# Four weight loads on ScalarE's queue and an input norm on VectorE alone, in the first stage of a two-layer hybrid attention trunk

## The chip, the cores and the metric

The kernel runs on one core of a Trainium2 chip. The metric is the device time of one execution in microseconds, and the median of several executions stands for a kernel. One execution was also taken by the hardware profiler; it has a time of its own beside its span (from the first to the last instruction on the core).

## The reference

The reference computes a two-layer trunk over 512 latent tokens and 256 context tokens of width 2048. What matters here is the head of layer 0:

```python
mod = silu_c @ w_mod[l] + b_mod[l]                     # c -> shift, scale, gate
shift, scale, gate = jnp.split(mod[:, None, :], 3, axis=-1)
h = rmsnorm(x, norm_g[l]) * (1.0 + scale) + shift       # the same for the context tokens, with c_ctx
u = h @ e_w_in[i]                                       # input projection, then the mixers
...
x = x + gate * (y @ w_o[l])
```

So no column of `h` can be made before the piece of `mod` that shifts and scales it, and `w_mod` is large: the shift and scale parts of layer 0 alone are 2048 x 4096 floats (33.6 MB).

## The kernel before, in words

Activations lie transposed: 16 chunks `k` of 128 features, each a tile of 128 partitions by 768 tokens (512 latent, 256 context). Every fp32 product is made of three matmuls on split operands: `wsplit` casts a piece of weights to a high part `wh` on ScalarE (L265), and VectorE makes the rest, `wl` (L224, the function `sub`); `make_h` does the same with an activation, giving `h` and `l`.

The first stage, which the change touches, works through eight groups `g` of 256 modulation columns:

- `mod_first(g)` loads the weights of group `g` in 11 pieces (`mraw`, L147; ten of 384 KB and one of 256 KB), multiplies each on TensorE into a bank (L151), copies the bank (L157, ScalarE), adds the four row strips on TensorE (L160), and `mod_finish` writes the columns `modc` on VectorE (L125, L129).
- `make_h(0, k, ...)` for the two chunks `k = 2g, 2g+1`: `xn = xT[k] * rs0` (L353), then the shift and scale on ScalarE (L358, makes `h`) and on VectorE (L361, in place in `xn`), then `l` (L224). In L353 GpSimd (POOL) does the ten chunks with `k % 3` not zero, VectorE (DVE) the six others. There are three buffers for `xn`, so `xn` of chunk `k` needs the `l` of chunk `k-3` to be done.
- The projection of four blocks of 128 output columns (`start_cols`) runs along with it, chunk by chunk: `mm_step` (L284, L285, L287). TensorE's order is written out by hand: in each pass `g` of the loop stand eight `mm_step`s; behind the first one group `g+1` is finished and its two `h` are begun, and behind each of the last four stand the matmuls of 3, 3, 3 and 2 pieces of group `g+2`. I call these four places the slots of a group.

Every load is issued by SP, the common queue (`nc.sync`), and SP issues in order: an issue that waits for a buffer holds all behind it. A scheduler orders the instructions of the engines other than TensorE. The `mraw` pieces lie in two kinds of buffers. Groups 0 to 4 use a pool of 32 tiles (`hslot`) that are free at the start. The later pieces of groups 5 and 6 use the tiles of the pool `s3` in which the inputs `xT[2]` to `xT[11]` lie at the start (`slot`); such a piece can be loaded only when L353 has read its `xT[k]`. The scheduler set these pieces early among the loads of groups 1 to 5.

The four weight blocks are loaded by `start_loads(k)` in two halves, `k = 0` and `k = 8`, four loads of 512 KB each (three `wraw`, and one into the buffer `macc`), L274:

```python
            if g == 2:
                with tc.issue_after(last_raw[0].ins):
                    start_loads(8)
```

Behind the stage come the heads of layer 0. There VectorE also sums further modulation columns (L179, `mod_later`), whose loads (L172) are on SP too.

Of the kernel before, what the change touches and what calls it, by code (L numbers as in the profile page):

```python
# [12 lines left out]
ALU = mybir.AluOpType  # L13
# [4 lines left out]
P = 128  # L18
# [23 lines left out]
def trunk_kernel(ctx: ExitStack, tc: tile.TileContext, T):  # L42
    nc = tc.nc
# [21 lines left out]
    def slot(name):  # L65
        return sp["s3"].tile([P, TOK], F32, tag="s3", name=name)
# [10 lines left out]
    def tmp(name):  # L77
        return sp["tm"].tile([P, TOK], F32, tag="tmp", name=name)

    def hslot(name, dt=F32R):  # L80
        return hp.tile([P, TOK], dt, tag="hT", name=name)
# [50 lines left out]
    last_raw = [None]  # L132

    def mod_first(g):

        acc = pst.tile([P, 512], F32, name="T")
        for r0 in range(0, 32, 3):
            n = min(3, 32 - r0)

            i = r0 // 3  # L140
            if i < (11, 11, 11, 11, 11, 6, 4, 3)[g]:
                raw = hslot("mraw0", F32)
            elif g == 7 and i > 8:
                raw = wp.tile([P, 1024], F32, name="mraw", bufs=2)
            else:
                raw = slot("mraw0")
            last_raw[0] = nc.sync.dma_start(raw[:, :n * 256], T["wm0"][g][:, r0 * 256:(r0 + n) * 256])  # L147
            for i in range(n):
                sec, at = divmod(r0 + i, NCH)
                j = at % 4  # L150
                nc.tensor.matmul(acc[32 * j:32 * j + 32, 256 * sec:256 * sec + 256], lhsT=sil[:, at, :],  # L151
                                 rhs=raw[:, 256 * i:256 * i + 256], start=(at < 4), stop=(at >= NCH - 4),
                                 tile_position=(0, 32 * j))
            if r0 + n < 32:
                yield
        asb = sp["ep"].tile([P, TOK], F32, name="e")[:, 0:512]
        nc.scalar.copy(asb, acc)  # L157
        yield
        for i in range(4):
            nc.tensor.matmul(acc[:, 2 * i:2 * i + 2], lhsT=asb[:, P * i:P * i + P], rhs=sel, start=True, stop=True)  # L160
        for sec in range(2):
            mod_finish(0, 2 * g + NCH * (1 - sec), 2, acc[:, 4 * sec:4 * sec + 4].rearrange("p (c v) -> p c v", c=2))
        yield
# [28 lines left out]
    def shift(l, k, v):  # L192
        return modc[l][:, k, v:v + 1]

    def ascale(l, k, v):
        return modc[l][:, NCH + k, v:v + 1]
# [26 lines left out]
    def sub(o, a, h):  # L223
        nc.vector.tensor_tensor(o, a, h.bitcast(F32), op=ALU.subtract)  # L224
# [19 lines left out]
    def rstd_cols(accs, ts, dim, name, bank=jbank):  # L244

        mp = bank()
        steps = [(a, t) for a in accs for t in ts]
        for i, (a, t) in enumerate(steps):
            nc.tensor.matmul(mp[:, 2 * t:2 * t + 2], lhsT=a[:, P * t:P * t + P], rhs=ones[:, 0:2],  # L249
                             start=(i == 0), stop=(i == len(steps) - 1))  # L250
        rs = sm.tile([P, 12], F32, name=name, bufs=2)
        n = 2 * len(ts)
        nc.scalar.activation(rs[:, :n], mp[:, :n], AF.Sqrt, bias=epsc, scale=1.0 / dim)
        nc.vector.reciprocal(rs[:, :n], rs[:, :n])
        return rs


    def wsplit(rv, nk):

        res = []  # L260
        for k0 in range(0, nk, 4):
            n = min(4, nk - k0)
            wh = wp.tile([P, 4, P], F32R, name="wh", bufs=4)
            wl = wp.tile([P, 4, P], F32R, name="wl", bufs=4)
            nc.scalar.copy(wh[:, :n, :], rv[:, k0:k0 + n, :])  # L265
            sub(wl[:, :n, :], rv[:, k0:k0 + n, :], wh[:, :n, :])
            res += [(wh[:, i, :], wl[:, i, :]) for i in range(n)]
        return res

    def wraw(w, col, k0, nk, raw=None):  # L270

        if raw is None:
            raw = wp.tile([P, 1024], F32, name="wraw", bufs=3)
        nc.sync.dma_start(raw[:, :nk * P], w[col // P][:, k0 * P:(k0 + nk) * P])  # L274
        return raw[:, :nk * P].rearrange("p (k c) -> p k c", k=nk)

    def mm_step(lat, cx, wk, xk, first, last, opens=True, closes=True, at=(0, 512)):


        wh, wl = wk  # L280
        xh, xl = xk
        regs = [(lat, *at)] + ([(cx, 512, 768)] if cx is not None else [])
        for o, c0, c1 in regs:
            nc.tensor.matmul(o, lhsT=wh, rhs=xh[:, c0:c1], start=first and (opens or o is lat), stop=False)  # L284
            nc.tensor.matmul(o, lhsT=wh, rhs=xl[:, c0:c1], start=False, stop=False)  # L285
        for o, c0, c1 in regs:
            nc.tensor.matmul(o, lhsT=wl, rhs=xh[:, c0:c1], start=False, stop=last and (closes or o is lat))  # L287

    def proj(w, col, xs=None, lat_only=False, at=(0, 512)):
        xs = hT if xs is None else xs  # L290
        n = len(xs)
        lat = psj.tile([P, 512], F32, name="J")[:, :at[1] - at[0]]
        cx = None if lat_only else psj.tile([P, 512], F32, name="J")[:, :256]
        for k0 in range(0, n, 8):
            nk = min(8, n - k0)
            ws = wsplit(wraw(w, col, k0, nk), nk)
            for i in range(nk):
                mm_step(lat, cx, ws[i], xs[k0 + i], k0 + i == 0, k0 + i == n - 1, at=at)
        return lat, cx
# [7 lines left out]
    for k in range(NCH):  # L307
        xk = hslot("xT", F32) if k == 0 else tmp("xT") if k == 1 else slot("xT") if k < 12 else (oslot if k < 14 else sgslot)("xT")
# [41 lines left out]

    def make_h(l, k, xk, rs, xn, first):

        (nc.gpsimd if k % 3 else nc.vector).tensor_tensor(xn, xk, rs, op=ALU.mult)  # L353
        h = hslot(f"h{l}_{k}")
        lo = hslot(f"l{l}_{k}")
        for v, c0, c1 in halves:
            a = ascale(l, k, v) if first == "norm" else 1.0
            nc.scalar.activation(h[:, c0:c1], xn[:, c0:c1], AF.Identity, bias=shift(l, k, v), scale=a)  # L358
        for v, c0, c1 in halves:
            if first == "norm":  # L360
                nc.vector.tensor_scalar(xn[:, c0:c1], xn[:, c0:c1], ascale(l, k, v), shift(l, k, v),  # L361
                                        op0=ALU.mult, op1=ALU.add)
            else:
                nc.vector.scalar_tensor_tensor(lo[:, c0:c1], xn[:, c0:c1], shift(l, k, v), h.bitcast(F32)[:, c0:c1],  # L364
                                               op0=ALU.add, op1=ALU.subtract)
        if first == "norm":
            sub(lo, xn, h)
        return h, lo


    w = T["ew"]
    s_start = sbanks()
    o_start = pso.tile([P, 512], F32, name="O")
    start_cols = (A_K0, A_Q0, A_V0, E_G0)
# [5 lines left out]
    raws = [None] * 4  # L380

    def start_loads(k):

        for i in range(4):
            raw = sm.tile([P, 2, 512], F32, name="macc", bufs=1).rearrange("p a b -> p (a b)") if i == 3 else None
            raws[i] = wraw(w, start_cols[i], k, 8, raw)

    def two_h(g):
        for k in (2 * g, 2 * g + 1):
            hs[k] = make_h(0, k, xT[k], rs0, tmp("xn"), "norm")  # L390
# [3 lines left out]
    with tc.manual_schedule(engines={mybir.EngineType.PE}):  # L394
        start_loads(0)
        for _ in mod_first(0):
            pass
        two_h(0)
        nxt = mod_first(1)
        for _ in range(11):  # L400
            next(nxt)
        for g in range(NCH // 2):
            for n in range(8):
                k, i = 2 * g + n // 4, n % 4
                if k % 4 == 0:
                    ws4[i] = wsplit(raws[i][:, k % 8:k % 8 + 4, :], 4)
                mm_step(*start_ps[i], ws4[i][k % 4], hs[k], k == 0, k == NCH - 1, opens=(i % 2 == 0), closes=(i % 2 == 1))
                if n == 0 and nxt is not None:
                    for _ in nxt:
                        pass  # L410
                    two_h(g + 1)
                    nxt = mod_first(g + 2) if g < NCH // 2 - 2 else None
                if n >= 4 and nxt is not None:
                    for _ in range((3, 3, 3, 2)[n - 4]):
                        next(nxt)
            if g == 2:
                with tc.issue_after(last_raw[0].ins):
                    start_loads(8)
    with tc.issue_after(last_raw[0].ins):
        load_cs(64)  # L420
    xT = None
# [302 lines left out]
    w = T["ow"]  # L724
# [6 lines left out]
    for k in range(NCH):  # L731
        xk = slot("xk")
# [65 lines left out]
    for g in range(2):  # L798
# [9 lines left out]
        rs = rstd_cols((sq,), range(6), P, "rsx", bank)  # L808
# [262 lines left out]
```

## Time and profile before

| what | us |
|---|---|
| median of 3 runs | 2517.13 |
| lowest and highest run | 2510.58, 2518.85 |
| the profiled execution, its own time | 2515.64 |
| its span | 2513.9 |
| TensorE busy | 2408.1 (96%) |
| VectorE busy | 1570.2 (62%) |
| ScalarE busy | 1011.7 (40%) |
| GpSimd busy | 247.8 (10%) |

The profiled execution's time and its span differ by 1.74 us. A row of the timeline has the start, the busy time, the engine, the line, the operation with its output and inputs, a count of merged instructions, and in brackets the engine's idle time before it and what ended it. A row of the waits has who waited for whom, the total, the number of waits and the longest. A row of a table by stretches has the stretch, its length, the busy time of TensorE, its weight loads, VectorE, ScalarE and GpSimd with counts, the granted TensorE clock, the busy share of the 16 DMA engines, and GB/s.

### The profile page before, as it was taken

To read this page: it belongs to the slowest core of one execution; us is meant where nothing else is said; L and a number is where in the kernel's file an instruction comes from. 1 tells how busy PE (TensorE), PEld (TensorE's weight loads), DVE (VectorE), ACT (ScalarE), POOL (GpSimd) and SP (SyncE) were. 2 spreads that over 40 slices of the span, in tenths; PEclk is the share of its full clock that TensorE was granted. 3 is DMA by queue.
4 is the path that set the end of the run, shared out by engine and by line. 5 is a ranking of instruction groups with operands and counts; after the bars stand their busy time and mean duration, and the time that the engine had idled before them with its cause. 6 is when DMAs were issued, how large, how long until landed. Compare 5 with 4: busy or idle time off the path is not lost.

```text
span 2513.9 us, 36308 instructions
## 1 busy us (share of the span) xinstructions
PE 2408.1 (96%) x14234; PEld 2077.1 (83%) x14234; DVE 1570.2 (62%) x2796; ACT 1011.7 (40%) x1964; POOL 247.8 (10%) x160
## 2 busy tenths in 40 slices
PE   3898999999999999999989999899999999999998
PEld 1677888888888899989878888688888888888787
DVE  4358667556965787887566664757545336776534
ACT  3234555444454334323342222444434334554434
POOL 1111001001000011010001012200001010100010
PEclk8999999999999999999999999899999999999999
DMA  8853111111312343443325545425422221222234
GB/s 305 302 179 100 43 57 56 50 57 57 109 58 72 100 144 113 142 164 111 134 96 199 188 170 184 146 92 191 150 72 84 69 95 56 64 93 68 97 118 151
DMA packets 97931, 297.48 MB, mean 118 GB/s; under 512 B 11488, under 2 KB 12512, under 8 KB 97760
## 3 DMA queue, kind: packets, MB, share of 16 engines
q1 hardware_dynamic: 97760, 295.16, 34.7%
q8 instruction: 112, 1.84, 0.3%
q14 instruction: 59, 0.48, 0.1%
HBM read 269.16 MB, written 25.95 MB: 117 GB/s over the span
## 4 chain that ended last, share of the span: by engine, by line
PE 87%; DVE 6%; DMA 3%; issue 2%; ACT 1%; SPq 0%; ACTq 0%; DVEq 0%
PE J L284 22%; PE J L287 22%; PE J L285 22%; PE O L563 6%; PE S L505 4%; PE T L548 3%; PE S L501 3%; DMA mraw<-in_wm_dram 2%; PE T L151 1%; DVE macc L179 1%; DVE l L364 1%; PE J L187 1%; DVE wl L224 1%; PE T L249 1%; PE T L229 1%
## 5 line engine op out<-in xcount | busy, mean ns | idle before, releaser
L284 PE MATMUL J<-h,wh 128*128 128x512 f32 (+1 forms) x2224 | 789.0, 356 | 9.3 <-DVE sg L493 3.2
L285 PE MATMUL J<-l,wh 128*128 128x512 f32 (+1 forms) x2224 | 762.5, 353 | 3.6 <-DVE l L364 3.6
L287 PE MATMUL J<-h,wl 128*128 128x512 f32 (+1 forms) x2224 | 704.3, 355 | 9.2 <-DVE wl L224 9.2
L265 ACT CAST wh<-wraw 128x512 fp32r<-128x512 f32 x492 | 304.1, 620 | 682.1 <-PE J L285 581.3
L224 DVE TENSOR_TENSOR wl<-wraw,wh 128x512 fp32r<-128x512 f32 x500 | 363.7, 731 | 317.7 <-ACT wh L265 307.1
L284 PEld LDWEIGHTS J<-h,wh 128*128 128x128 f32 x2224 | 421.3, 189 | 94.3 <-issue 8.2
L285 PEld LDWEIGHTS J<-l,wh 128*128 128x128 f32 x2224 | 421.9, 190 | 56.7 <-DVE l L364 4.8
L287 PEld LDWEIGHTS J<-h,wl 128*128 128x128 f32 x2224 | 386.4, 190 | 44.1 <-DVE wl L224 12.4
L179 DVE SCALAR_TENSOR_TENSOR macc<-mraw,silc,macc 128x512 f32<-128x512 f32 x420 | 317.2, 787 | 34.6 <-DMA mraw<-in_wm_dram 31.9
L284 PE MATMUL J<-yh,wh 128*128 128x512 f32 (+1 forms) x800 | 275.3, 351 | 4.7 <-ACT yh L469 4.7
L285 PE MATMUL J<-yl,wh 128*128 128x512 f32 (+1 forms) x800 | 271.7, 350 | 1.0 <-DVE yl L224 0.9
L287 PE MATMUL J<-yh,wl 128*128 128x512 f32 (+1 forms) x800 | 253.6, 349 | 0.2 <-DVE wl L224 0.2
L517 DVE TENSOR_REDUCE nb<-S 128x1 f32<-128x768 f32 (+3 forms) x208 | 166.2, 799 | 140.0 <-PE S L505 73.0
L552 ACT CAST pth<-T 128x256 fp32r<-128x256 f32 (+2 forms) x288 | 125.0, 450 | 190.4 <-PE T L548 186.6
L284 PEld LDWEIGHTS J<-yh,wh 128*128 128x128 f32 x800 | 149.9, 189 | 31.6 <-ACT yh L469 5.5
L224 DVE TENSOR_TENSOR ptl<-T,pth 128x256 fp32r<-128x256 f32 (+2 forms) x288 | 144.2, 514 | 49.1 <-ACT pth L552 47.3
L285 PEld LDWEIGHTS J<-yl,wh 128*128 128x128 f32 x800 | 150.5, 189 | 22.3 <-DVE yl L224 3.1
L524 ACT ACTIVATE e<-S,nb 128x256 f32<-128x256 f32 (+3 forms) x144 | 104.3, 724 | 156.4 <-DVE nb L517 90.5
L287 PEld LDWEIGHTS J<-yh,wl 128*128 128x128 f32 x800 | 140.4, 189 | 13.2 <-DVE wl L224 0.5
L431 POOL TENSOR_TENSOR r<-r,cos 128x512 f32<-128x512 f32 x31 | 44.3, 1428 | 792.1 <-DVE t L430 736.2
L548 PE MATMUL T<-identr,e 128*128 128x128 f32 x784 | 116.3, 275 | 2.9 <-DVE e L534 2.6
L548 PEld LDWEIGHTS T<-identr,e 128*128 128x128 f32 x784 | 95.2, 142 | 16.7 <-issue 2.8
(283 smaller groups left out, 3143.7 us busy)
## 6 DMA issues: line engine op xcount, KB each, us to landing
mraw<-in_wm_dram SPq DMA_DIRECT2D x128, 512.0 KB, 3.7
wraw<-in_ew_dram SPq DMA_DIRECT2D x102, 512.0 KB, 3.7
wraw<-in_ow_dram SPq DMA_DIRECT2D x64, 512.0 KB, 3.6
wraw<-in_wo_dram SPq DMA_DIRECT2D x62, 512.0 KB, 3.8
mraw<-in_wm_dram SPq DMA_DIRECT2D x80, 384.0 KB, 7.4
xT<-in_xT_dram SPq DMA_DIRECT2D x16, 384.0 KB, 7.6
res<-in_xT_dram SPq DMA_DIRECT2D x16, 384.0 KB, 4.3
xad<-nx SPq DMA_DIRECT2D x16, 384.0 KB, 2.7
```

Of the source, the lines that this page charges most:

```text
L179: nc.vector.scalar_tensor_tensor(macc[:, v, :], rv[:, i, :], sc, macc[:, v, :], op0=ALU.mult, op1=ALU.add)
L224: nc.vector.tensor_tensor(o, a, h.bitcast(F32), op=ALU.subtract)
L265: nc.scalar.copy(wh[:, :n, :], rv[:, k0:k0 + n, :])
L284: nc.tensor.matmul(o, lhsT=wh, rhs=xh[:, c0:c1], start=first and (opens or o is lat), stop=False)
L285: nc.tensor.matmul(o, lhsT=wh, rhs=xl[:, c0:c1], start=False, stop=False)
L287: nc.tensor.matmul(o, lhsT=wl, rhs=xh[:, c0:c1], start=False, stop=last and (closes or o is lat))
L505: nc.tensor.matmul(S[:, 512:end], lhsT=q, rhs=k[:, 128 * lo:128 * hi], start=(i == 0), stop=(i == n - 1 and not masks))
L517: nc.vector.tensor_reduce(nb, S, axis=AX.X, op=ALU.max, negate=True)
L524: nc.scalar.activation(e, S, AF.Exp, bias=nb, scale=1.0 if scale is None else scale, accum_out=den)
L548: nc.tensor.transpose(out=tp[:, 128 * (b - b0):128 * (b - b0) + 128], in_=e[:, 128 * b:128 * b + 128], identity=ident)
L552: nc.scalar.copy(ph, tv)
L563: nc.tensor.matmul(o, lhsT=v[:, cols[i]], rhs=pt[part][:, i, :], start=(n == 0), stop=(n == len(steps) - 1))
```

## The change

It has three parts. Both calls of `start_loads` issue their four loads on ScalarE's queue. The second call no longer waits for the last piece of the modulation weights that was issued ahead of it. And L353 of the first stage (`l == 0`) is done by VectorE for all 16 chunks.

```diff
-    def wraw(w, col, k0, nk, raw=None):
+    def wraw(w, col, k0, nk, raw=None, queue=None):
...
-        nc.sync.dma_start(raw[:, :nk * P], w[col // P][:, k0 * P:(k0 + nk) * P])
+        (queue or nc.sync).dma_start(raw[:, :nk * P], w[col // P][:, k0 * P:(k0 + nk) * P])
...
-        (nc.gpsimd if k % 3 else nc.vector).tensor_tensor(xn, xk, rs, op=ALU.mult)
+        (nc.gpsimd if l and k % 3 else nc.vector).tensor_tensor(xn, xk, rs, op=ALU.mult)
...
-            raws[i] = wraw(w, start_cols[i], k, 8, raw)
+            raws[i] = wraw(w, start_cols[i], k, 8, raw, nc.scalar)
...
-                with tc.issue_after(last_raw[0].ins):
-                    start_loads(8)
+                start_loads(8)
```

The scheduler answers with another order on SP. This is SP's queue behind the loads of group 1, whose last piece is `mraw_468`; `mraw_1012` and `mraw_1023` are pieces of group 5 that go into the tiles of `xT[4]` and `xT[5]`, and `mraw_546` is the first piece of group 2:

```order
 L147 DMA mraw_468<-in_wm_dram 128x512
 L147 DMA mraw_1012<-in_wm_dram 128x768
+L147 DMA mraw_1023<-in_wm_dram 128x768
 L147 DMA mraw_546<-in_wm_dram 128x768
 L147 DMA mraw_551<-in_wm_dram 128x768
```

The piece for the tile of `xT[5]` moved ahead of the eleven loads of group 2. This is SP's queue between group 2 (last piece `mraw_614`) and group 3 (first piece `mraw_676`); `mraw_1028` goes into the tile of `xT[6]`, and `mraw_1132`, of group 6, into that of `xT[7]`:

```order
 L147 DMA mraw_609<-in_wm_dram 128x768
 L147 DMA mraw_614<-in_wm_dram 128x512
-L147 DMA mraw_1023<-in_wm_dram 128x768
 L147 DMA mraw_1028<-in_wm_dram 128x512
+L147 DMA mraw_1132<-in_wm_dram 128x768
 L147 DMA mraw_676<-in_wm_dram 128x768
 L147 DMA mraw_681<-in_wm_dram 128x768
```

The piece for `xT[7]` moved ahead of group 3, behind which it stood. And this is SP's queue between group 4 (last piece `mraw_890`) and the first pieces of group 5; `mraw_1153` and `mraw_1158` go into the tiles of `xT[10]` and `xT[11]`:

```order
 L147 DMA mraw_885<-in_wm_dram 128x768
 L147 DMA mraw_890<-in_wm_dram 128x512
-L274 DMA wraw<-in_ew_dram 128x1024 x3
-L274 DMA macc<-in_ew_dram 128x1024
 L147 DMA mraw_1153<-in_wm_dram 128x768
+L147 DMA mraw_1158<-in_wm_dram 128x768
 L147 DMA mraw_960<-in_wm_dram 128x768
 L147 DMA mraw_965<-in_wm_dram 128x768
```

The four weight loads are gone from there, and the piece for `xT[11]` moved ahead of group 5. On VectorE, this is the work around the finish of group 1 in the kernel before (`xn_491` is chunk 2, `xn_500` chunk 3):

```order
L125 TENSOR_TENSOR modc0_193<-T_417,bmod_174 128x4 x2
L129 SCALAR_TENSOR_TENSOR modc0_193<-modc0_193,vcol_173 128x4
L361 TENSOR_SCALAR xn_491<-xn_491,modc0_193 128x512
L361 TENSOR_SCALAR xn_491<-xn_491,modc0_193 128x256
L224 TENSOR_TENSOR l0_2_494<-xn_491,h0_2_493 128x768
L361 TENSOR_SCALAR xn_500<-xn_500,modc0_193 128x512
L361 TENSOR_SCALAR xn_500<-xn_500,modc0_193 128x256
L224 TENSOR_TENSOR l0_3_503<-xn_500,h0_3_502 128x768
```

And the same place now, where `xT_216` is `xT[4]` and `xT_221` is `xT[5]`:

```order
L353 TENSOR_TENSOR xn_633<-xT_216,e_276 128x768
L125 TENSOR_TENSOR modc0_193<-T_417,bmod_174 128x4 x2
L129 SCALAR_TENSOR_TENSOR modc0_193<-modc0_193,vcol_173 128x4
L361 TENSOR_SCALAR xn_491<-xn_491,modc0_193 128x512
L361 TENSOR_SCALAR xn_491<-xn_491,modc0_193 128x256
L224 TENSOR_TENSOR l0_2_494<-xn_491,h0_2_493 128x768
L361 TENSOR_SCALAR xn_500<-xn_500,modc0_193 128x512
L353 TENSOR_TENSOR xn_642<-xT_221,e_276 128x768
L361 TENSOR_SCALAR xn_500<-xn_500,modc0_193 128x256
L224 TENSOR_TENSOR l0_3_503<-xn_500,h0_3_502 128x768
```

The two L353 that GpSimd had stand among VectorE's instructions, that of chunk 5 behind the finish of group 1. Last, ScalarE's queue around the finish of group 2, where the second half of the weights is issued:

```order
L358 ACTIVATE h0_5_644<-xn_642,modc0_193 128x512
L358 ACTIVATE h0_5_644<-xn_642,modc0_193 128x256
L265 CAST wh_750<-wraw_327 128x512
L274 DMA wraw_896<-in_ew_dram 128x1024
L265 CAST wh_785<-wraw_329 128x512
L274 DMA wraw_898<-in_ew_dram 128x1024
```

Each load stands behind the cast that read its buffer last and ahead of the next cast. It waits for VectorE's `wl` of that buffer as well.

## The prediction

> **What bounds the kernel now.** I read the page's head first, then the stretches of the first stage, then SP's waits, then the timeline of TensorE and VectorE there.
>
> ```profile
> PE 2408.1 (96%) x14234; PEld 2077.1 (83%) x14234; DVE 1570.2 (62%) x2796; ACT 1011.7 (40%) x1964; POOL 247.8 (10%) x160
> 40.00:60.00 20.00, 8.60 (x60) 2.54 (x60) 4.83 (x10) 3.09 (x5) 1.80 (x1) 0.66 0.69 242
> 60.00:80.00 20.00, 18.56 (x152) 11.31 (x149) 6.43 (x10) 3.10 (x5) 2.01 (x1) 1.00 1.00 376
> 100.00:120.00 20.00, 13.99 (x94) 7.37 (x93) 3.21 (x5) 0.52 (x2) 1.80 (x1) 0.74 0.86 319
> 120.00:140.00 20.00, 20.00 (x151) 14.82 (x150) 10.79 (x20) 8.37 (x14) 2.01 (x1) 1.00 0.80 293
> ```
>
> TensorE bounds the kernel as a whole, so only time that TensorE loses or wins counts. In the stage that the change touches it loses time at two places, around 50 and around 105 us, and there its granted clock is low too (0.66 and 0.74). What ends those waits is SP's queue:
>
> ```profile
> SPq L147 <- DVE xn L353: 9.3, 1, 9.3
> SPq L147 <- DVE xn L353: 10.7, 1, 10.7
> 48.04 0.95 DVE L353 TENSOR_TENSOR xn<-xT,e 128x768 f32<-128x768 f32 x1
> 49.06 19.29 SPq L147 DMA_DIRECT2D mraw<-in_wm_dram  x24
> 100.97 0.96 DVE L353 TENSOR_TENSOR xn<-xT,e 128x768 f32<-128x768 f32 x1
> ```
>
> The first two rows are SP's waits in the stretches 39 to 50 and 90 to 104 us: SP stood 9.3 and 10.7 us at a piece of group 5 or 6 whose tile still held `xT[3]` or `xT[9]`, until VectorE's L353 of that chunk ended at 49.0 and 101.9. The loads of groups 1 and 4 stood behind. The row at 49.06 shows the opposite case: 24 issues in 19.3 us are the blocked piece, the 11 of group 1, the piece for `xT[4]`, and all 11 of group 2, so group 2 was issued by 68.35, before anything of it was needed.
>
> What a blocked group costs is read from VectorE's finish of each group and TensorE's matmuls on its pieces:
>
> ```profile
> 44.53 0.23 DVE L125 TENSOR_TENSOR modc<-T,bmod 128x4 f32<-128x4 f32 x2 [9.78 <-PE T L160]
> 66.88 0.23 DVE L125 TENSOR_TENSOR modc<-T,bmod 128x4 f32<-128x4 f32 x2 [16.57 <-PE T L160]
> 82.16 0.23 DVE L125 TENSOR_TENSOR modc<-T,bmod 128x4 f32<-128x4 f32 x2 [7.80 <-PE T L160]
> 97.45 0.23 DVE L125 TENSOR_TENSOR modc<-T,bmod 128x4 f32<-128x4 f32 x2 [2.09 <-PE T L160]
> 121.88 0.23 DVE L125 TENSOR_TENSOR modc<-T,bmod 128x4 f32<-128x4 f32 x2 [18.64 <-PE T L160]
> 137.17 0.23 DVE L125 TENSOR_TENSOR modc<-T,bmod 128x4 f32<-128x4 f32 x2 [2.04 <-PE T L160]
> 168.57 0.23 DVE L125 TENSOR_TENSOR modc<-T,bmod 128x4 f32<-128x4 f32 x2 [2.04 <-PE T L160]
> 71.00 1.48 PE L151 MATMUL T<-mraw,sil 128*32 128x256 f32 x18
> 88.95 1.48 PE L151 MATMUL T<-mraw,sil 128*32 128x256 f32 x18
> 106.36 1.95 PE L151 MATMUL T<-mraw,sil 128*32 128x256 f32 x12 [4.71 <-DMA mraw<-in_wm_dram]
> 112.84 2.00 PE L151 MATMUL T<-mraw,sil 128*32 128x256 f32 x18
> ```
>
> These are the finishes of groups 0, 1, 2, 3, 4, 5 and 7. A group whose loads came ahead takes 15.28 us (66.88 to 82.16), 15.29 (82.16 to 97.45) or 15.29 (121.88 to 137.17). The one that was blocked, group 4, takes 24.43 (97.45 to 121.88): 9.15 more. The loss is complete by the second slot: 112.84 + 2.00 is 17.39 after the finish ahead of it, where 88.95 + 1.48 is 8.27, so 9.12.
>
> **The change part by part.** First, which pieces block after the change. A load into the tile of `xT[k]` can go when L353 of chunk `k` is done. In the new order the pieces for `xT[5]`, `xT[7]` and `xT[11]` stand ahead of groups 2, 3 and 5, and those L353 stand on VectorE behind the finishes of groups 1, 2 and 4. Their place is that of chunks 3 and 9 above, between the two L361 of the chunk before. The end of L353 there is 101.93 - 97.45 = 4.48 us after the finish. Nothing can make it earlier: it needs that finish's L361 and `l` to free an `xn` buffer. In the kernel before GpSimd did these three, later still, but SP had the groups' loads out by then:
>
> ```profile
> 70.21 2.01 POOL L353 TENSOR_TENSOR xn<-xT,e 128x768 f32<-128x768 f32 x1 [18.03 <-DVE l L224]
> 125.22 2.01 POOL L353 TENSOR_TENSOR xn<-xT,e 128x768 f32<-128x768 f32 x1 [20.04 <-DVE l L224]
> ```
>
> Group 2: SP reaches its new blocker around 60 (13 issues after 49.06 instead of 24, at 19.3 / 24 = 0.8 us), waits until 66.88 + 4.5 = 71.4, and only then issues the eleven loads; TensorE wants the first three at 71.00. That is group 4's situation to the row, so I take its whole loss, +9.15. From below the loss is at least the idle time ahead of the first matmul, 4.71; from above I have only the 9.15 itself and what competes for the transfer. Group 3: the same, +9.15. Group 5: only six of its pieces stand behind the blocker, the other five having been loaded into `xT` tiles; but the loss arises in the first two slots, which are those six. Seven instead of twelve transfers run together, so I take +8.0, between 4.71 and 9.15. Groups 1 and 4 are blocked at the same chunks (3 and 9) as before: 0.
>
> Second, the first four weight loads, 2.1 MB. They leave SP's queue between `tri` and group 0 and start with the kernel.
>
> ```profile
> 16.00:18.00 2.00, 0.00 (x0) 0.00 (x0) 1.79 (x3) 1.56 (x3) 0.00 (x0) 1.00 1.03 415
> 20.00:22.00 2.00, 0.00 (x0) 0.00 (x0) 1.79 (x3) 1.56 (x3) 0.00 (x0) 1.00 0.20 37
> 24.00:26.00 2.00, 0.00 (x1) 0.01 (x1) 1.10 (x4) 0.41 (x1) 0.00 (x0) 1.00 1.01 403
> 19.61 2.96 SPq L274 DMA_DIRECT2D wraw<-in_ew_dram  x3
> 22.61 0.97 SPq L274 DMA_DIRECT2D macc<-in_ew_dram  x1
> 42.73 0.58 ACT L157 COPY e<-T 128x512 f32<-128x512 f32 x1 [10.63 <-PE T L151]
> ```
>
> The transfers were full at 415 GB/s while the inputs came, so the weights push these back by what they take themselves, 2.1 MB / 403 GB/s = 5.2 us, and group 0's loads then start where the weights' issues stood. The dip at 20 us comes from the six small loads behind the inputs, which stay. Group 0's finish is the end of the same bytes: 0, with -5.2 (the weights cost nothing early) and +4.0 (SP's 2.96 + 0.97 of issuing turn out to have been hidden, and the inputs' delay is not) as ends. The Trainium skill, page "DMA: Bandwidth & Descriptors", section "Issuing engines are not separate DMA queues", states that transfers begun by different engines run on the same 16 DMA engines and interleave, and that a second issuing engine saves only the sequencer's issue time. By that rule this term is 0 too, where a reader who counts a second queue as more bandwidth would write -5.2. The norm's factors come some 5 us later, with the inputs (4 casts and 4 `wl` now stand among the squares); VectorE idled 9.78 us ahead of group 0's finish and ScalarE 10.63 ahead of its copy at 42.73, which covers it; without that slack it would be +5.2. TensorE's six L229 behind group 0's first three pieces lie in the same slack.
>
> Third, the second half of the weights. ScalarE issues it behind the casts for chunk 4, while group 3's blocked loads come:
>
> ```profile
> 86.05 0.62 ACT L265 CAST wh<-wraw 128x512 fp32r<-128x512 f32 x1 [0.94 <-PE S L285]
> 88.71 0.62 ACT L265 CAST wh<-wraw 128x512 fp32r<-128x512 f32 x1 [2.04 <-PE S L285]
> 88.56 2.91 DVE L224 TENSOR_TENSOR wl<-wraw,wh 128x512 fp32r<-128x512 f32 x2
> 68.18 0.90 DVE L361 TENSOR_SCALAR xn<-xn,modc 128x512 f32<-128x512 f32 x2 [0.95 <-ACT h L358]
> 70.00 2.38 DVE L361 TENSOR_SCALAR xn<-xn,modc 128x512 f32<-128x512 f32 x2
> ```
>
> Each issue waits for a `wl` and holds the next cast, but these casts wait 2 us for TensorE anyway, so ScalarE loses nothing; if TensorE no longer held them, it would be about 0.7 us each. One load of 512 KB (1.3 us at 403 GB/s) lands among the pieces that TensorE awaits, the others follow the slots: +1.3, ends 0 and 5.2. Gone from SP behind group 4, they free nothing, since group 5 now waits for its own blocker. The removed order behind the last piece costs and gives nothing: the buffer decides.
>
> Fourth, ten L353 move to VectorE, 10 x 0.96 = 9.6 us of work. They fit in its gaps, as at 70.00, where a pair of L361, 0.90 us of work in the row at 68.18, spans 2.38; cover gone, each would add 0.96.
>
> The sum: 9.15 + 9.15 + 8.0 + 0 + 1.3 = 27.6 us. Does it reach the end? Behind the stage VectorE sets the pace for a while:
>
> ```profile
> 180.00:200.00 20.00, 17.04 (x80) 12.86 (x78) 18.65 (x22) 12.63 (x21) 6.67 (x4) 1.00 0.35 113
> 200.00:220.00 20.00, 14.00 (x85) 12.78 (x86) 19.68 (x27) 7.78 (x13) 3.36 (x2) 0.91 0.24 80
> 166.06 14.34 SPq L172 DMA_DIRECT2D mraw<-in_wm_dram  x5
> ```
>
> TensorE loses 3.0 and 6.0 us there. If VectorE did those sums (L179) in the new waits, up to 9 us came back. But their loads stand on SP behind group 7's, from 166 us on, so they shift along. All of the 27.6 goes through: 2515.64 + 27.6 = 2543.2. The profiled execution lies 1.5 us below the median of the three runs and inside their range, so I leave it there: 2543.
>
> **The rivals.** (a) Faster: the early weights ride for nothing and the three pieces hardly block, because VectorE frees the tiles before SP gets to them. Then the 5.2 of group 0 is left: 2515.6 - 5.2 = 2510.4. It decides where a blocked group costs less than 1.7 us, that is, where L353 ends within that of SP's arrival. Against it stand the share of 1.03 while the inputs come, and L353's place behind the finish. (b) First arrival only: the slots need three pieces at a time, and the rest comes as fast as TensorE eats it, so that each group costs the idle 4.71: 2515.6 + 14.1 = 2529.8. Against it: in group 4 the clock fell and the second slot was late as well. (c) Contention: all four weight loads go ahead of group 3's pieces (+5.2 instead of +1.3) and group 0 is 4.0 to 5.2 late because ScalarE's queue takes a share of the transfers: 2543.2 + 3.9 + 4.6 = 2551.7. For it: both fall into times of full transfers. (d) Given back: 9 us return behind the stage, 2534. (e) The change does nothing that counts: the blocked pieces are hidden behind group 1's transfers, about 2516. Against it: SP is at the blocker at about 60, and L353 ends at 71.4.
>
> **How the numbers follow.** Forecast 0.70, its own range 2536 to 2550 (group terms of 7 to 9.15, weights 0 to 5.2); (a) 0.04, (b) 0.08, (c) 0.08, (d) 0.05, (e) 0.05. From (b) to (c) lie 0.91 of it, and I widen (c) by a microsecond: 2529 to 2553. 0.3% is 7.6 us, about what a measurement of this kernel can tell from no change. Faster by more 0.04 from (a), within it 0.05 from (e), slower 0.91.
>
> **What would show it.** In the new profile the finishes of groups 1 to 5 should lie 24 to 26 us apart, 23 for group 5, with SP waiting for VectorE's L353 four or five times for some 7 to 11 us, GpSimd idle until the heads, and two or three more dips of the granted clock to 0.5 before 170 us. Group 0's finish should stay at 44 to 45, and that of group 7 should be at 196. I am wrong if the finishes of groups 2 and 3 stay 15 apart, if group 0's moves by more than 3, or if the time from group 7's finish to the end shrinks by more than 5.

## The result, and the profile after

The changed kernel takes 2545.19 us (median of 4 runs, 2544.20 to 2545.93), the kernel before 2515.07 (4 runs, 2510.58 to 2518.85): 1.012 times the time, with a 95% interval of 1.0101 to 1.0139. The profiled execution took 2545.78 us at a span of 2543.9, against 2515.64 and 2513.9, so the two profiles show the whole difference, 30.1 us.

These are VectorE's finishes of groups 0 to 7 in the changed kernel, from the timeline:

```profile
42.00 0.23 DVE L125 TENSOR_TENSOR modc<-T,bmod 128x4 f32<-128x4 f32 x2 [1.59 <-PE T L160]
64.15 0.23 DVE L125 TENSOR_TENSOR modc<-T,bmod 128x4 f32<-128x4 f32 x2 [15.38 <-PE T L160]
88.31 0.23 DVE L125 TENSOR_TENSOR modc<-T,bmod 128x4 f32<-128x4 f32 x2 [17.38 <-PE T L160]
114.50 0.23 DVE L125 TENSOR_TENSOR modc<-T,bmod 128x4 f32<-128x4 f32 x2 [2.09 <-PE T L160]
139.04 0.23 DVE L125 TENSOR_TENSOR modc<-T,bmod 128x4 f32<-128x4 f32 x2 [17.75 <-PE T L160]
163.18 0.23 DVE L125 TENSOR_TENSOR modc<-T,bmod 128x4 f32<-128x4 f32 x2 [2.09 <-PE T L160]
179.79 0.23 DVE L125 TENSOR_TENSOR modc<-T,bmod 128x4 f32<-128x4 f32 x2 [9.83 <-PE T L160]
195.09 0.23 DVE L125 TENSOR_TENSOR modc<-T,bmod 128x4 f32<-128x4 f32 x2 [2.04 <-PE T L160]
```

Groups 2, 3 and 5 now last 24.16, 26.19 and 24.14 us, where they lasted 15.28, 15.29 and 15.29. Groups 1 and 4 are as long as before (22.15 and 24.54). Group 7's finish is 26.52 us later than at 168.57. Next, the stretches of the table, whose columns are those of the section on the profile before; the last two lie behind the stage:

```profile
40.00:60.00 20.00, 9.40 (x64) 2.68 (x62) 6.20 (x12) 3.09 (x5) 0.00 (x0) 0.57 0.77 269
60.00:80.00 20.00, 13.34 (x82) 8.14 (x80) 5.79 (x11) 3.10 (x5) 0.00 (x0) 0.83 0.59 212
100.00:120.00 20.00, 18.02 (x114) 11.27 (x114) 6.62 (x13) 4.95 (x8) 0.00 (x0) 0.82 0.67 257
120.00:140.00 20.00, 15.22 (x103) 8.69 (x104) 1.61 (x5) 1.16 (x2) 0.00 (x0) 0.74 0.68 250
200.00:220.00 20.00, 17.97 (x95) 14.55 (x93) 18.78 (x26) 7.81 (x15) 3.75 (x3) 1.00 0.42 131
220.00:240.00 20.00, 12.93 (x77) 11.04 (x78) 19.68 (x24) 8.37 (x14) 5.73 (x4) 0.92 0.17 53
```

From 60 to 80 us TensorE is busy 13.34 us instead of 18.56, with the transfers at 212 GB/s instead of 376: the DMA engines stand idle four tenths of the time (share 0.59 instead of 1.00) while TensorE waits for data. In the 40 us behind the stage it loses 2.03 + 7.07 = 9.1 us, as before (3.0 + 6.0); in the stretches that lie 26.5 us behind those of the kernel before, 206.5 to 226.5 and 226.5 to 246.5 us, it is 2.96 + 6.14, again 9.1. The waits of SP in the stretches 52 to 75, 80 to 97 and 125 to 150 us (who waited for whom, total, number, longest) show why:

```profile
SPq L147 <- DVE xn L353: 13.6, 1, 13.6
SPq L147 <- DVE xn L353: 14.9, 1, 14.9
SPq L147 <- DVE xn L353: 15.2, 1, 15.2
```

And the timeline of group 2, with SP's issues and TensorE's matmuls on the pieces:

```profile
67.67 0.95 DVE L353 TENSOR_TENSOR xn<-xT,e 128x768 f32<-128x768 f32 x1
68.69 3.65 SPq L147 DMA_DIRECT2D mraw<-in_wm_dram  x8
73.16 1.96 PE L151 MATMUL T<-mraw,sil 128*32 128x256 f32 x12 [4.82 <-DMA mraw<-in_wm_dram]
76.59 1.07 PE L151 MATMUL T<-mraw,sil 128*32 128x256 f32 x6 [1.47 <-DMA mraw<-in_wm_dram]
79.81 1.48 PE L151 MATMUL T<-mraw,sil 128*32 128x256 f32 x18
```

SP stands 13.6 us at the piece for the tile of `xT[5]`, until VectorE's L353 of chunk 5 ends at 68.62, goes on at 68.69, and TensorE, which wanted group 2's first pieces at about 68.3, gets them at 73.16 after 4.82 us of idling. The matmuls then run at half speed (1.96 us for 12, where 1.48 is for 18), at a granted clock of 0.50 from 73.0 to 75.2 us. The shift of 26.52 us stays 26.5 to 27.0 until 1217 us of the kernel before (by the starts of GpSimd's rows; only around 880 us it is 24.5 to 25.1); between there and 1308 another 3.1 us arise, in the heads of layer 0.

### The profile page after: what moved, and what is told of

It reads as the page before. It is cut to its first block, busy times and chain, and to the rows that moved or that the text cites. A ratio compares the mean times of both kernels' runs of the same rounds, so it can differ in the third digit from the quotient of the medians.

```text
span 2543.9 us, 36289 instructions
## 1 busy us (share of the span) xinstructions
PE 2416.2 (95%) x14234; PEld 2078.4 (82%) x14234; DVE 1572.3 (62%) x2806; ACT 1012.6 (40%) x1964; POOL 228.1 (9%) x150
## 4 chain that ended last, share of the span: by engine, by line
PE 87%; DVE 6%; DMA 4%; issue 2%; ACT 1%; SPq 0%; POOL 0%; ACTq 0%; DVEq 0%; POOLq 0%
PE J L284 22%; PE J L285 22%; PE J L287 22%; PE O L562 5%; PE S L504 4%; PE T L547 3%; PE S L500 3%; DMA mraw<-in_wm_dram 2%; PE T L151 1%; DVE macc L179 1%; DVE l L364 1%; PE J L187 1%; PE T L249 1%; DVE wl L224 1%; DMA xT<-in_xT_dram 1%
```

## The experiments

All kernels differ from one of the two by a few lines. A "held" piece is one that `issue_after` puts behind the last piece of a group on SP, so that the group's loads go first. Line numbers are up to 4 higher in those kernels (L149, L153 and L355 for L147, L151 and L353). The lengths of the groups come from the finishes in one profile each; the times are medians, beside runs of the kernel before on the same chip (2515.86 us for e1 to e4, 2516.25 for e5 to e8, 2515.95 for e9 and e10).

| kernel | time, ratio and interval | groups 1, 2, 3, 4, 5 (us) | group 7 ends |
|---|---|---|---|
| before | 2515.07 | 22.35, 15.28, 15.29, 24.43, 15.29 | 168.57 |
| changed | 2545.19, 1.0120 [1.0101, 1.0139] | 22.15, 24.16, 26.19, 24.54, 24.14 | 195.09 |
| e1 queue alone | 2515.10, 0.9994 [0.9985, 1.0004] | 22.11, 15.34, 15.28, 24.67, 15.29 | 166.88 |
| e2 norm alone | 2546.61, 1.0121 [1.0106, 1.0136] | 22.11, 25.05, 24.50, 23.93, 24.17 | 196.37 |
| e3 three held | 2517.77, 1.0006 [0.9996, 1.0016] | 22.09, 15.34, 18.95, 24.49, 15.28 | 170.84 |
| e4 one held | 2540.61, 1.0094 [1.0079, 1.0110] | 22.02, 15.29, 26.03, 23.72, 23.94 | 186.48 |
| e5 e3, a weight load later | 2513.86, 0.9990 [0.9980, 0.9999] | 21.99, 15.30, 15.29, 24.52, 15.28 | 166.85 |
| e6 five held | 2507.10, 0.9962 [0.9947, 0.9977] | 16.69, 15.30, 16.98, 16.20, 15.28 | 154.92 |
| e7 before, two held | 2502.10, 0.9944 [0.9929, 0.9959] | 14.69, 15.30, 15.29, 15.29, 15.30 | 152.91 |
| e8 queue alone, two held | 2504.77, 0.9951 [0.9936, 0.9966] | 18.48, 15.35, 15.28, 20.82, 15.29 | 161.02 |
| e9 changed, a weight load later | 2542.40, 1.0099 [1.0082, 1.0116] | 21.81, 24.68, 24.46, 24.83, 24.48 | 197.04 |
| e10 norm alone, five held | 2499.46, 0.9931 [0.9916, 0.9946] | 16.21, 15.34, 15.28, 15.29, 15.30 | 152.57 |

**Either half alone.** e1 has the weights on ScalarE's queue and L353 shared as before; e2 has L353 on VectorE alone and the weights on SP.

```diff
 # e1, against the changed kernel
-        (nc.gpsimd if l and k % 3 else nc.vector).tensor_tensor(xn, xk, rs, op=ALU.mult)
+        (nc.gpsimd if k % 3 else nc.vector).tensor_tensor(xn, xk, rs, op=ALU.mult)
 # e2, against the kernel before
-        (nc.gpsimd if k % 3 else nc.vector).tensor_tensor(xn, xk, rs, op=ALU.mult)
+        (nc.gpsimd if l and k % 3 else nc.vector).tensor_tensor(xn, xk, rs, op=ALU.mult)
```

> The weight loads are on ScalarE's queue as in the changed kernel, L353 is shared with GpSimd as before; SP's pieces for xT[5], xT[7] and xT[11] stand behind groups 2, 3 and 5 again. Theory A (SP is held at these three pieces, and that alone costs): the eight finishes lie as before, 22.2, 15.3, 15.3 to 17 (group 3 shares the transfers with the weights), 24.4, 15.3, 16.1, 15.3 apart, with the first at 42.0 as in the changed kernel; 2513 us, within 4 of before. Theory B (the loads on ScalarE's queue cost, by contention): 2530 or more, with the finishes of groups 2 to 5 about 24 apart.

> L353 is VectorE's for all 16 chunks, all weight loads are on SP as before; SP's order has the three pieces ahead of groups 2, 3 and 5. Theory A: first finish at 44.5, then 22.3, 24.2, 24.4, 24.4, 24.1, 16.6, 15.3: 27 us above before by group 7's finish and, with the instruction order behind the stage that it shares with the changed kernel (+3), 2545. Theory B: 2515. Theory C (VectorE's ten further L353 are the cost, by delaying h and l) gives 2541 here too and is told apart by the next run.

e1 is the kernel before in time and in its groups, e2 the changed one. So the whole loss in time belongs to the edit of L353. What that edit does, VectorE's additional work or the order it leads to on SP, these two don't tell.

**The order undone, VectorE's work kept.** e3 is the changed kernel with the three pieces put back behind groups 2 and 3 and behind the first six of group 5; e4 puts back the first alone.

```diff
+    piece, hold = {}, {(5, 9): (2, 10), (6, 4): (3, 10), (6, 8): (5, 5)}    # e4: (5, 9) alone
...
-            last_raw[0] = nc.sync.dma_start(raw[:, :n * 256], T["wm0"][g][:, r0 * 256:(r0 + n) * 256])
+            with tc.issue_after(piece[hold[g, i]].ins) if (g, i) in hold else nullcontext():
+                last_raw[0] = piece[g, i] = nc.sync.dma_start(raw[:, :n * 256], T["wm0"][g][:, r0 * 256:(r0 + n) * 256])
```

> The changed kernel, both edits kept, but the pieces for xT[5], xT[7] and xT[11] are held behind the last loads of group 2, of group 3 and of group 5's first six, where they stood before. Theory A: the finishes lie 22.2, 15.3, 15.3 to 17, 24.5, 15.3, 16.5, 15.3 apart; 2513 to 2516. Theories B and C: no gain, 2541 to 2545.

> The changed kernel with only the piece for xT[5] held behind group 2. Theory A: the finish of group 2 comes 8.9 us earlier (15.3 behind that of group 1 instead of 24.2), groups 3 and 5 stay at 26.2 and 24.1; 2536. Theories B and C: 2545.

e4's group 2 is back at 15.29 and groups 3 and 5 are not; e3 is back at the time of the kernel before, with VectorE doing all L353. That shows the mechanism: a piece that waits for L353, at the head of SP's queue. The time of e4 missed its forecast all the same: its profiled execution took 2536.37 us, as expected, but the three others took 2540.53 to 2541.22, so that its median fell by 4.6 us where group 7's finish came 8.6 earlier. What the slower three lost, no profile shows. And e3's 2517.77 lies 1.8 us above its range, because group 3 of e3 still lasts 18.95 us. SP's wait in that stretch, and the issue of a weight load from the view of the transfers (its last column is the time from issue to landing):

```profile
SPq L149 <- DMA wraw<-in_ew_dram: 10.9, 1, 10.9
```
```profile
wraw<-in_ew_dram ACTq DMA_DIRECT2D x1, 512.0 KB, 3.3
```

And the timeline of ScalarE's issue, SP's next issues, and TensorE's matmuls on the pieces that these bring:

```profile
86.04 0.33 ACTq L276 DMA_DIRECT2D wraw<-in_ew_dram  x1
89.45 2.13 SPq L149 DMA_DIRECT2D mraw<-in_wm_dram  x4
94.54 1.27 PE L153 MATMUL T<-mraw,sil 128*32 128x256 f32 x10 [1.77 <-DMA mraw<-in_wm_dram]
```

SP waited 10.9 us for a weight load of the other queue, issued at 86.04 and landed 3.3 us later, and only then issued group 3's last two pieces. The wait began at 89.45 - 10.9 = 78.55, so for 7.5 us of it the load had not even been issued: it stands behind a cast in ScalarE's queue. The two loads share no buffer. What they share stands in the built program: every load counts its landing on one of eight semaphores, which are given out in turn, in program order, over both queues, and it waits until the load before it on its semaphore has landed. In the changed kernel itself, SP's row 75 (the ninth piece of group 3) and ScalarE's row 49 (the first of the later weight loads) are

```
75 L147 DMA mraw_728<-in_wm_dram 128x768 [waits DMAHW0_49,PE_49]
49 L274 DMA wraw<-in_ew_dram 128x1024 [waits DMAHW0_49,DVE_49]
```

and its trace has the same wait: SP's from 98 to 101 us, the weight load in the view of the transfers, and the timeline of the two issues.

```profile
SPq L147 <- DMA wraw<-in_ew_dram: 3.0, 1, 3.0
```
```profile
wraw<-in_ew_dram ACTq DMA_DIRECT2D x1, 512.0 KB, 6.6
```
```profile
93.74 0.37 ACTq L274 DMA_DIRECT2D wraw<-in_ew_dram  x1
100.44 0.82 SPq L147 DMA_DIRECT2D mraw<-in_wm_dram  x2
```

93.74 + 6.6 is 100.34, and SP goes on at 100.44.

**The shared semaphore.** e5 is e3, and e9 the changed kernel, with that first weight load one cast further down ScalarE's queue. It then takes another semaphore, whose next user is a piece of group 4.

```diff
+    cast = []
...
-            nc.scalar.copy(wh[:, :n, :], rv[:, k0:k0 + n, :])
+            cast.append(nc.scalar.copy(wh[:, :n, :], rv[:, k0:k0 + n, :]))
...
-                start_loads(8)
+                with tc.issue_after(cast[-3].ins):
+                    start_loads(8)
```

Here `cast[-3]` is ScalarE's cast of the second weight block; the load stood behind that of the first.

> The changed kernel with the three pieces held behind groups 2, 3 and 5, and the first of the four later weight loads placed one cast further down ScalarE's queue; TensorE's order is then the kernel before's. With the three pieces held, group 3 still took 18.95 us instead of 15.3. Theory (a shared counter): the loads of both queues take eight completion semaphores in turn, and a load waits until the one before it on its semaphore has landed; there the first later weight load has the semaphore of group 3's piece before the last, so that piece waits for ScalarE's load (issued at 86.0, landed at about 89.4; SP went on at 89.45). One cast later it takes a semaphore whose next user stands behind group 3: group 3 goes to 15.3, the time to about 2514 us (2512.5 to 2515.5). Rival (transfer time): the weights' bytes take the engines from group 3's pieces; the same bytes still come in the same stretch, group 3 stays at 18 to 19 us and the time at about 2518. Rival (VectorE later at L353 than GpSimd was): nothing of it changes here either, 18 to 19 us and 2518.

> The changed kernel with one difference: the first of the four later weight loads stands one cast further down ScalarE's queue. SP's order is the changed kernel's, with the three pieces ahead of groups 2, 3 and 5, so these stay at 24 to 25 us. The load now takes a semaphore whose next user is a piece of group 4. If the shared semaphore is what made group 3 cost 10.9 us more instead of the 9.15 of a blocked group, group 3 goes from 26.2 to 24.3-24.6 us, 1.6 to 1.9 less; if it was transfer time or VectorE, it stays at 26.2. TensorE's order in the heads of layer 0 (where the changed kernel's 3.1 us beyond the stage arose, from 1217 to 1308 us) is the kernel before's again: if that order is their cause, the time behind group 7's finish goes from 2348.8 to about 2345.5 us and the kernel to about 2540 us (2538 to 2542); if they are scatter of the granted clock, it is 2543.5.

Both went as the semaphore has it. In e5 group 3 takes 15.29 us. In e9, with SP's order untouched, it takes 24.46 instead of 26.19 (e2, with no weight load on ScalarE's queue, had 24.50), and SP's waits from 77 to 100 us name VectorE and pieces of its own, no weight load:

```profile
SPq L147 <- DVE xn L355: 15.5, 1, 15.5
SPq L147 <- DMA mraw<-in_wm_dram: 2.2, 2, 1.6
```

e9 was to settle the 3 us behind the stage too, and doesn't: its time behind group 7's finish is 2544.3 - 197.04 = 2347.3 us, between the changed kernel's 2348.8 and the 2345.3 of the kernel before, and its median of 2542.40 between the two forecasts.

**What is left in the queue.** Groups 1 and 4 are long in both kernels. e6 is the changed kernel with all five pieces held, e7 the kernel before with its two, e8 is e1 with those two, e10 is e2 with five.

```diff
+    piece, hold = {}, {(5, 7): (1, 10), (5, 9): (2, 10), (6, 4): (3, 10), (6, 6): (4, 10), (6, 8): (5, 5)}    # e6, e10
+    piece, hold = {}, {(5, 7): (1, 10), (6, 6): (4, 10)}    # e7, e8
```

> The changed kernel with five pieces held: those for the buffers of input chunks 3, 5, 7, 9 and 11, each behind the group it stood ahead of (1 to 5). If an in-order queue behind a waiting piece is all that makes a group last 22 to 26 us, groups 1, 2, 4 and 5 go to 13.5 to 15.5 us each and group 3 to about 19 (its weights' semaphore is as before): 2545.2 - 8 - 8.9 - 7.2 - 9.2 - 8.9 = about 2503 us (2499 to 2507), faster than both kernels. Rival (groups 1 and 4 are long for another reason, in both kernels: transfers or casts): they stay at 22 and 24.5 us and the time at 2518 to 2520. Rival (given back behind the stage, where weights or VectorE are not ready earlier): the finishes come earlier, but the time stays above 2510.

> The kernel before with the two pieces held that stand ahead of its groups 1 and 4 (for the buffers of chunks 3 and 9). If the queue's order is the cause, its group 1 goes from 22.35 to 13.5-15.5 us and its group 4 from 24.43 to 15.3: 2515.9 - 7 to 8.9 - 9.1 = about 2498 us (2495 to 2502). If these two were long for another reason, 2516; if it is given back behind the stage, 2505 to 2514 with the earlier finishes.

> The same two pieces held, with the first blocks' weights on ScalarE's queue (the one half of the change that cost nothing by itself, 2515.1 against 2515.9). The later weight loads' first one has a semaphore whose next user stands behind group 3, so group 3 takes 15.3 us: about 2497.5 us, within 2 us of the same kernel with its weights on the common queue. If moving them relieves the common queue once nothing else holds it, group 0 or 1 ends 1 to 3 us earlier and it comes to 2494 to 2496; if the weights' transfers then collide with group 1's or 3's pieces, 2499 to 2504.

> L353 on VectorE alone, the weights on the common queue as in the kernel before, and the five pieces held behind groups 1 to 5. No weight load shares a semaphore with a waiting one on the other queue and no piece stands ahead of its group: by the theory groups 2, 3, 4 and 5 take 15.1 us each and group 1 14 to 15, group 7 ends at 152 to 154 and the time is that of the kernel before with two pieces held, 2502 us (2499 to 2506, with up to 3 us for another order of TensorE behind the stage). If VectorE's ten additional L353 cost something of their own once nothing waits on SP (10 x 0.96 = 9.6 us at most), groups last 15.5 to 17 and it comes to 2506 to 2512.

All four beat both kernels. e10 has the lowest median, but its interval overlaps e7's, so these two are not told apart. The finishes of e10's groups 0 to 5, and 7:

```profile
42.99 0.23 DVE L125 TENSOR_TENSOR modc<-T,bmod 128x4 f32<-128x4 f32 x2 [6.80 <-PE T L162]
59.20 0.23 DVE L125 TENSOR_TENSOR modc<-T,bmod 128x4 f32<-128x4 f32 x2 [9.43 <-PE T L162]
74.54 0.23 DVE L125 TENSOR_TENSOR modc<-T,bmod 128x4 f32<-128x4 f32 x2 [8.55 <-PE T L162]
89.82 0.23 DVE L125 TENSOR_TENSOR modc<-T,bmod 128x4 f32<-128x4 f32 x2 [2.09 <-PE T L162]
105.11 0.23 DVE L125 TENSOR_TENSOR modc<-T,bmod 128x4 f32<-128x4 f32 x2 [8.51 <-PE T L162]
120.41 0.23 DVE L125 TENSOR_TENSOR modc<-T,bmod 128x4 f32<-128x4 f32 x2 [2.04 <-PE T L162]
152.57 0.23 DVE L125 TENSOR_TENSOR modc<-T,bmod 128x4 f32<-128x4 f32 x2 [2.03 <-PE T L162]
```

Groups 2 to 5 take 15.28 to 15.34 us with VectorE doing every L353, so that half of the change costs nothing of its own. The half with ScalarE's queue does cost, in the groups, once SP isn't held elsewhere. e8's group 3 took 15.28 as expected, but I had not asked what stood behind it: the weight load's semaphore was next used by a piece ahead of group 4, and group 4 took 20.82:

```profile
SPq L149 <- DMA wraw<-in_ew_dram: 9.5, 1, 9.5
```

That is SP's wait in e8 from 75 to 100 us. In e6 the same kind of wait, 9.0 us, stands in group 3, which takes 16.98. In time, e6's interval lies just above e10's, while e8's overlaps e7's although its group 7 ends 8.1 us later: the time behind group 7 was 2343.1 us in e8 and 2348.0 in e7. The times of e6 and e7 lie 0.1 us above my ranges, e8's 7.3 us above its forecast of 2497.5 and 0.8 above the dearest case that I gave it. Group 1 took 16.69, 18.48 and 16.21 us in e6, e8 and e10, more than I expected, and e6's group 4 took 16.20. A sixth piece, for the tile of `xT[2]`, stood ahead of group 1 in these kernels and was not held; SP waited for the L353 of chunk 2 there, 4.1 us in e6 and 5.8 in e8, and issued group 1's loads only behind it. No run takes that piece away.

## Why the prediction was right, and where it was not

The forecast was 2543 us in a range of 2529 to 2553; measured was 2545.19. By its own steps, in microseconds and from the two profiles where no experiment is named:

| step | predicted | measured |
|---|---|---|
| group 2 blocked | +9.15 | +8.88 |
| group 3 blocked | +9.15 | +9.17 in e9; +10.90 in the changed kernel |
| group 5 blocked | +8.0 | +8.85 |
| groups 1 and 4 | 0 | -0.20, +0.11 |
| early weight loads, group 0's finish | 0 | -2.53 |
| later weight loads | +1.3 | +1.73 (26.19 - 24.46, in group 3) |
| ten L353 on VectorE | 0 | 0 (e10) |
| given back behind the stage | 0 | 0 |
| group 6; behind group 7 | not named | +0.5; +3.5 |

- The main step held. A group behind a piece that waits for L353 costs what group 4 cost before. e4 and e3 show it by taking the pieces away one and three at a time, and e2 shows that it needs nothing from the weights. Rivals (a) and (e), the blocked pieces costing little or nothing, and (b), 4.71 each, fall by the same numbers.
- SP came to the blockers earlier than I said (at 68.62 - 13.6 = 55.0 us for group 2, where I had about 60), so its waits were 13.6 to 15.9 us instead of some 7 to 11. That changed no cost, since the cost was read from when the tile comes free: L353 of chunk 5 ended 68.62 - 64.15 = 4.47 us after the finish, where I had 4.48.
- Group 5 was mis-sized. I took 8.0 because only six of its pieces stand behind the blocker. It measured 8.85, and 9.19 in e9. My reading, which no run tests, is that the first six pieces fill the first two slots and that the loss is complete there; that they share the transfers with fewer others brought nothing measurable.
- The later weights came out near the number by luck, through a mechanism that I had not seen. The +1.3 stood for bytes that compete with group 3's. The runs showed a wait: SP's piece waited for ScalarE's load to land, because the two loads had the same semaphore. The bytes alone cost nothing that e1 or e9 shows. Rival (c), contention, falls with it.
- Early weights: the profile pair has group 0's finish 2.53 us earlier, but that can't be put down to the queue. The eight kernels with these loads on ScalarE's queue have it at 42.00 to 44.41 us, the four with them on SP at 42.99 to 45.52, and e1's time is that of the kernel before to a thousandth. (The finish at 42.00 lies outside the 44 to 45 that I named as a sign, though within 3 us.) The cover that I counted on held, but narrowly: VectorE's idle time ahead of group 0's finish went from 9.78 to 1.59 us. The rule cited from the Trainium skill, "DMA: Bandwidth & Descriptors", "Issuing engines are not separate DMA queues", agrees with the runs: a second issuing engine gave no more bandwidth (365 to 387 GB/s from 6 to 12 us with both queues' loads under way, 366 to 410 with SP alone), so the -5.2 of a reader who counts it double did not come. What the runs add is that the two issuing queues are not independent of each other in this program either.
- Nothing came back behind the stage (9.1 us lost there, 9.0 before), so rival (d) falls.
- The 3.1 us between 1217 and 1308 us were not in the sum. TensorE's order there differs from the kernel before's, by the scheduler, but the order alone does not make them. e4 runs TensorE in the very order of the changed kernel. From the last L432 ahead of that stretch to the first L700 behind it (L431 and L699 in the changed kernel, L433 and L701 in e4), these are the kernel before, the changed kernel and e4:

```profile
1203.78:1313.84 110.06, 101.06 (x604) 87.85 (x603) 61.94 (x143) 46.14 (x106) 4.92 (x3) 0.98 0.33 107
1230.52:1343.75 113.23, 103.84 (x604) 90.04 (x603) 61.78 (x143) 46.24 (x106) 4.95 (x4) 0.95 0.32 105
1222.50:1332.84 110.34, 101.59 (x603) 87.94 (x602) 61.80 (x143) 46.37 (x106) 4.92 (x4) 0.98 0.32 106
```

  e4 is through in 110.34 us, as the kernel before is. In the changed kernel TensorE is busy 2.8 us longer, at a granted clock of 0.95 instead of 0.98. Why the clock was lower in that execution stays open, and so does whether the order has a share in it: the same stretch took 110.3 to 113.2 us in the changed kernel, e2, e4 and e6, which have one order there, 112.4 in e1, whose order is nearly theirs, and 109.0 to 110.7 in the seven other kernels. Over the whole way behind group 7's finish the single profiles scatter more than that, from 2342.8 (e10) to 2349.9 us (e2), and the orders overlap: e1 took 2344.3, the kernel before 2345.3.
- The total came closer than its terms. Group 0's -2.53 and the +3.5 behind group 7, neither of which was in the sum, nearly cancel. And one chance was booked wrongly: (a), at 2510.4, lies 5.2 us below the kernel before, inside the 7.6 us that I gave for no change.

## What to carry to other kernels

Moving an operation to another engine changed, through the scheduler, the order of a queue that the edit doesn't name (by which estimate of its own, the runs don't show). So look first at what now stands at the head of each in-order queue, when its buffer is released, and what it holds. One load that waited for a late release cost the group behind it 9 us, with the data engines idle four tenths of the time; with five such loads behind those that were needed sooner, the edit that had lost 1.2% ran 0.7% faster than the kernel before. That gain is the loads', not the edit's: the kernel before with its own two loads held back (e7) gained 0.6%, and the two intervals overlap. And a load on a second queue can still hold the first where both take their completion semaphores from one set, so read the waits in the built program, not the buffers alone.

## What I had not expected

The wait across queues. A load on ScalarE's queue held SP for 3.0 us in the changed kernel, 9.0 in e6, 9.5 in e8 and 10.9 in e3, with no buffer in common, and moving it by a single cast removed the delay of group 3 (18.95 to 15.29 us in e3 and e5). And a blocked group's loss hardly depended on how much stood behind the blocker: 8.65 to 9.19 us with six pieces (group 5 of the changed kernel, e2, e4 and e9), 8.88 to 9.77 with eleven (group 2 of the changed kernel, e2 and e9).
